# A conformer block in FP32-like precision: five FFN pairs and twelve down-projection tiles by Strassen's scheme

## The chip, the cores and the metric

The kernel runs on one core of a Trainium2 chip. The time is the device time of that core in microseconds for one execution; a run's number is the median of its executions. One execution of each kernel is also recorded by the hardware profiler, and all rows below are from that one. PE is TensorE, DVE is VectorE, ACT is ScalarE, POOL is GpSimd, SP is the engine that issues the DMAs.

## The reference

One layer: a conformer convolution mixer and then a gated conv-FFN, for one sequence of 1024 tokens by 1024 channels, FFN width 2816, all in float32. Cut to what matters:

```python
h = rmsnorm(x, norm_pre_mix) * (1 + sc_m) + sh_m
u = h @ w1 + b1;  a, gt = split(u);  u = a * sigmoid(gt)
u = causal_dwconv(u, dw_w) + dw_b                 # width 31
u = silu(layernorm(u, ln_g, ln_b));  y = u @ w2 + b2
x = x + gt_m * rmsnorm(y, norm_post_mix)
h = rmsnorm(x, norm_pre_ffn) * (1 + sc_f) + sh_f
u = causal_dwconv(h @ w_up, f_dw_w) + f_dw_b      # width 3
gt, v = split(u);  y = (silu(gt) * v) @ w_down
out = x + gt_f * rmsnorm(y, norm_post_ffn)
```

## The kernel before, in words

The tokens are two blocks (0 and 1) of 512. Activations lie channels on partitions, a tile being 128 channels by 512 tokens. Every large product is three matmuls (`mm3`, L256 to L258; `mm3g`, L627 to L629): each operand is split into a high half (rounded, L242 on ScalarE or L244 on VectorE) and a low half (the rest, L245 on VectorE or GpSimd), and high x high, high x low and low x high are added in PSUM. A weight tile is loaded to `raw` (three buffers), split into `W` (four buffers), and used.

The program's order is: modulation vectors and pointwise1 of block 0 with part of block 1; the width-31 depthwise convolution of block 0 (`conv`: taps in PSUM on VectorE, L353; seven taps go by ScalarE products L347 and GpSimd additions L351); its layer norm; pointwise2 of block 0; a shared pointwise1 tile of block 1; the transposes and modulation of block 0 (`modulate_block`, L265). Then the FFN of block 0: 12 tile pairs up (`up_pair`: 48 matmuls, the width-3 convolution L526 to L528, gate L535 and L536), the down projection of these 12 (`down_half`, ci 0), 10 more pairs, and the down projection of those (ci 1) in two halves of the output channels. Between the two halves stand block 1's layer norm (`ln_center` L403 and on, `ln_rstd` L429 to L437, `ln_swish` L444), pointwise2 of block 1 with its residual and norm (`pointwise2`, L458 to L478), and, inside the second half, block 1's transposes. Block 1's convolution, all on VectorE, runs beside block 0's FFN.

Block 1's FFN goes in three chunks (8, 8 and 6 tiles): the pairs of a chunk (`up_pair` with low halves on VectorE), for every two of them the four sums and differences of hidden-tile quarters (`hid_pair`, L611 to L614 on GpSimd), and the down projection by Strassen's scheme with seven products in place of eight (`down_strassen`; weight combinations L691 on VectorE; accumulators in SBUF, L656).

Each engine takes its instructions in a fixed order that the build decides; an instruction that waits holds back those behind it on its engine. Tile pools release a buffer when its last reader is done.

## Time and profile before

| | |
|---|---|
| runs shown | 1096.85 us median (1096.79 to 1172.39) |
| the profiled execution | 1097.28 us; span 1095.5, so 1.8 us lie around it |
| PE busy | 1065.0 us, 97% |
| DVE busy | 817.3 us, 75% |
| POOL busy | 524.1 us, 48% |
| ACT busy | 500.4 us, 46% |
| mean granted PE clock | 0.991 |
| DMA | 139 MB, 36.9% of 16 engines' span |

How to read it: a share of the span says how long an engine worked, not whether others waited for it. The chain of work that ended last says what the end hung on, the waits say what an engine's idle time ended with, and the timeline gives start and length of single instructions (a row with a count is several in a run). Matmuls overlap in the records, so their pace is read from start to start.

### The profile page before, as it was taken

The page shows a single profiled execution, that of the slowest core. Times are in us where ns is not written, and L with a number is a line of the kernel's source. Part 1 is how long each engine was busy: PE and PEld are TensorE (multiplying, and loading weights), DVE is VectorE, ACT ScalarE, POOL GpSimd, SP SyncE. Part 2 cuts the span into 40 slices and gives each one's busy share as a digit, 9 for nine tenths or more (in the row PEclk, how much of TensorE's full clock was granted, in tenths as well). Part 3 has the DMA queues.
Part 4 walks back from the last instruction along what each step waited for, and adds up shares of the span by engine and source line. Part 5 has one row for each costly group of instructions (what it writes and reads, how often), then busy time and mean ns, then how long its engine had stood idle before and what let it go on. Part 6 is the DMA issues. An engine that isn't in the chain of part 4 may idle for free.

```text
span 1095.5 us, 13048 instructions
## 1 busy us (share of the span) xinstructions
PE 1065.0 (97%) x4786; PEld 841.9 (77%) x4786; DVE 817.3 (75%) x1103; ACT 500.4 (46%) x774; POOL 524.1 (48%) x420
## 2 busy tenths in 40 slices
PE   5999999999899999999999999999999999999995
PEld 3778876778688888888887788888887888878873
DVE  3499989534799999989978673786596555965687
ACT  3595555453644544333434442445445444343453
POOL 1398877544734444443344363433267024640464
PEclk9999999999899999999999999999999999999998
DMA  9951135443422223342243353567204322043022
GB/s 369 369 193 58 58 116 192 154 135 104 146 75 90 87 97 96 97 173 97 96 151 100 96 154 96 173 211 270 97 20 154 115 97 96 19 135 109 26 77 77
DMA packets 41832, 139.01 MB, mean 127 GB/s; under 512 B 4644, under 2 KB 4644, under 8 KB 41768
## 3 DMA queue, kind: packets, MB, share of 16 engines
q1 hardware_dynamic: 41768, 138.18, 36.9%
q8 instruction: 37, 0.61, 0.2%
q14 instruction: 27, 0.22, 0.1%
HBM read 129.77 MB, written 8.39 MB: 126 GB/s over the span
## 4 chain that ended last, share of the span: by engine, by line
PE 89%; DVE 5%; POOL 2%; DMA 1%; ACT 1%; issue 1%; SPq 0%; POOLq 0%; DVEq 0%; ACTq 0%
PE bank L256 26%; PE bank L257 26%; PE bank L258 26%; PE bank L628 2%; PE bank L629 2%; PE bank L627 2%; DVE W L245 1%; PE bank L265 1%; PE bank L178 1%; DMA Y<-in_mod_ch 1%; DVE Y L473 1%; PE cbank L149 1%; DVE yacc L656 1%; DVE R L691 1%; DMA x2d<-Y 0%
## 5 line engine op out<-in xcount | busy, mean ns | idle before, releaser
L256 PE MATMUL bank<-A,W 128*128 128x512 f32 x960 | 379.6, 398 | 0.3 <-ACT U L267 0.3
L257 PE MATMUL bank<-A,W 128*128 128x512 f32 x960 | 379.2, 395 | 0.0
L258 PE MATMUL bank<-A,W 128*128 128x512 f32 x960 | 378.9, 395 | 0.0
L245 POOL TENSOR_TENSOR W<-raw,W 128x1024 fp32r<-128x1024 f32 x99 | 244.8, 2473 | 272.5 <-ACT W L242 230.3
L353 DVE SCALAR_TENSOR_TENSOR cbank<-U,vecs,cbank 128x512 f32<-128x512 f32 x424 | 290.8, 747 | 9.0 <-ACT cbank L341 7.8
L256 PEld LDWEIGHTS bank<-A,W 128*128 128x128 f32 x960 | 180.9, 189 | 48.5 <-DVE cbank L353 1.7
L258 PEld LDWEIGHTS bank<-A,W 128*128 128x128 f32 x960 | 180.9, 188 | 43.6 <-issue 0.8
L257 PEld LDWEIGHTS bank<-A,W 128*128 128x128 f32 x960 | 180.8, 188 | 43.4 <-issue 1.1
L242 ACT ACTIVATE W<-raw 128x1024 fp32r<-128x1024 f32 x150 | 158.0, 1053 | 110.1 <-PE bank L258 72.7
L526 ACT ACTIVATE U<-bank,vecs 128x512 f32<-128x512 f32 x88 | 68.4, 778 | 194.3 <-PE bank L258 184.6
L527 DVE SCALAR_TENSOR_TENSOR U<-bank,vecs,U 128x511 f32<-128x511 f32 x88 | 65.4, 745 | 80.2 <-ACT U L526 80.0
L256 PE MATMUL bank<-W,A 128*128 128x512 f32 x304 | 121.1, 398 | 0.0
L257 PE MATMUL bank<-W,A 128*128 128x512 f32 x304 | 120.2, 395 | 0.0
L258 PE MATMUL bank<-W,A 128*128 128x512 f32 x304 | 118.9, 395 | 0.0
L532 POOL TENSOR_TENSOR U<-U,hv 128x2 f32<-128x2 f32 x44 | 12.7, 289 | 155.9 <-DVE U L527 153.0
L245 DVE TENSOR_TENSOR W<-raw,W 128x1024 fp32r<-128x1024 f32 x51 | 62.2, 1221 | 16.4 <-ACT W L242 16.3
L245 DVE TENSOR_TENSOR A<-U,A 128x512 fp32r<-128x512 f32 x73 | 67.3, 933 | 8.3 <-ACT A L242 7.7
L351 POOL TENSOR_TENSOR Q<-Q,Q 128x512 f32<-128x512 f32 x48 | 62.2, 1296 | 15.9 <-ACT Q L347 14.9
L256 PEld LDWEIGHTS bank<-W,A 128*128 128x128 f32 x304 | 57.2, 188 | 13.7 <-DVE U L536 0.2
L257 PEld LDWEIGHTS bank<-W,A 128*128 128x128 f32 x304 | 57.2, 188 | 13.6 <-issue 0.5
L258 PEld LDWEIGHTS bank<-W,A 128*128 128x128 f32 x304 | 57.2, 188 | 13.5
L528 DVE SCALAR_TENSOR_TENSOR U<-bank,vecs,U 128x510 f32<-128x510 f32 x88 | 65.3, 744 | 1.6
(147 smaller groups left out, 1208.1 us busy)
## 6 DMA issues: line engine op xcount, KB each, us to landing
raw<-in_wup SPq DMA_DIRECT2D x88, 512.0 KB, 3.2
raw<-in_w SPq DMA_DIRECT2D x40, 512.0 KB, 3.9
Y<-in_mod_hp SPq DMA_DIRECT2D x32, 512.0 KB, 5.9
raw<-in_wdn SPq DMA_DIRECT2D x22, 512.0 KB, 3.5
R<-in_wdn SPq DMA_DIRECT2D x20, 512.0 KB, 3.7
Af<-in_mod_ch SPq DMA_DIRECT2D x12, 512.0 KB, 10.2
Y<-in_x SPq DMA_DIRECT2D x8, 512.0 KB, 10.0
U<-in_x SPq DMA_DIRECT2D x16, 256.0 KB, 3.9
```

The costliest lines, as they stand in the source:

```text
L242: nc.scalar.activation(dst[:, 0], src, AF.Copy)
L245: split_lo[0] = lo.tensor_tensor(dst[:, 1], src, dst[:, 0].bitcast(F32), op=ALU.subtract)
L256: nc.tensor.matmul(o, l[0], r[0], start=start, stop=False)
L257: nc.tensor.matmul(o, l[0], r[1], start=False, stop=False)
L258: nc.tensor.matmul(o, l[1], r[0], start=False, stop=stop)
L351: nc.gpsimd.tensor_tensor(acp, acp, q, op=ALU.add)
L353: nc.vector.scalar_tensor_tensor(acc, ut[:, k:k + 512], tap(k), acc, op0=ALU.mult, op1=ALU.add)
L526: nc.scalar.activation(t[:, :512], bk, AF.Identity, bias=V("fb", i), scale=wk[2])
L527: nc.vector.scalar_tensor_tensor(t[:, 1:512], bk[:, 0:511], wk[1], t[:, 1:512], op0=ALU.mult, op1=ALU.add)
L528: nc.vector.scalar_tensor_tensor(t[:, 2:512], bk[:, 0:510], wk[0], t[:, 2:512], op0=ALU.mult, op1=ALU.add)
L627: nc.tensor.matmul(o, l[0], r[0], start=start, stop=False, skip_group_check=group)
L628: nc.tensor.matmul(o, l[0], r[1], start=False, stop=False, skip_group_check=group)
```

## The change

It has five parts. (1) The convolution of block 1 gives nine of its taps to ScalarE and GpSimd, and two of its eight channel tiles are asked for ahead of the rest. (2) Block 0's FFN runs its first 10 pairs as before; their down projection goes to DRAM (`down_spill` into `yd`). Block 1's layer norm, pointwise2 and the operands for what follows (`both_operands`) come right after. (3) Pairs 15 to 19 are computed once for both blocks by seven products of 1024 x 512 halves (`up_both`: 84 matmuls), where a second up projection in block 1 fell away; their outputs go to DRAM (`hd`). (4) Tiles 10 to 14, 20 and 21 of block 0 go to DRAM too, and all 12 come back into `hid_pair` and two chunks of `down_strassen`, which add to `yd`. (5) Four pairs of block 1 are computed ahead, and block 1's chunks reload what is stored.

Lines of the changed file stand some ten higher: L353 becomes L363, L256 to L258 become L264 to L266, L245 is L253, L244 is L252, L265 is L273, L437 is L447, L444 is L454, L478 is L488, L611 to L614 are L602 to L605, L627 to L629 are L618 to L620.

```diff
-CHUNKS = ((0, 12), (12, 22))
+NSTD = 10
+BOTH = range(15, 20)
+CHUNKS0 = ((10, 16), (16, 22))
+AHEAD = 4
+EARLY = 2
+POOL_TAPS1 = 9
...
+    def down_spill(lo, hi, h, hid, lo_eng, yd):
         n = hi - lo
...
         ys = [bank() for _ in range(NT)]
...
+        for q in range(n // 2):
+            ww = weights(wdn[h, :, (lo // 2 + q) * 1024:(lo // 2 + q + 1) * 1024], lo_eng)
             for t in range(NT):
...
+                for e in range(2):
...
+                    mm3(ys[t], (a[:, 0, ts], a[:, 1, ts]), (ww[:, 0, sl], ww[:, 1, sl]), kk == 0, kk == n - 1)
+                if q == n // 2 - 1:
+                    y = tU()[:, :512]
+                    nc.scalar.copy(y, ys[t])
+                    nc.sync.dma_start(yd[t * P:(t + 1) * P, h * 512:(h + 1) * 512], y)
...
+    def both_operands(h2, xs, keep):
...
...
+        B = {"B11": h2[:4], "B21": h2[4:], "B22": [], "B1": [], "B2": [], "B3": [], "B4": []}
+        for k in range(4):
+            h11, h21 = h2[k].bitcast(F32), h2[k + 4].bitcast(F32)
+            x12 = modulate_T(xs, s_f, sh_f, k, hi=None)
+            nc.sync.dma_start(keep[k], x12)
+            x22 = modulate_T(xs, s_f, sh_f, k + 4, hi=None)
+            B["B22"].append(operand(x22, V, True))
+            t1, t2, t3, t4 = [tU()[:, :512] for _ in range(4)]
+            V.tensor_tensor(t1, x12, h11[:, 0], op=ALU.subtract)
+            V.tensor_tensor(t1, t1, h11[:, 1], op=ALU.subtract)
+            G.tensor_tensor(t3, x22, x12, op=ALU.subtract)
+            V.tensor_tensor(t2, x22, t1, op=ALU.subtract)
+            G.tensor_tensor(t4, h21[:, 0], t2, op=ALU.subtract)
+            G.tensor_tensor(t4, t4, h21[:, 1], op=ALU.add)
+            for n, x, lo in (("B1", t1, V), ("B2", t2, V), ("B3", t3, V), ("B4", t4, G)):
+                B[n].append(operand(x, lo))
+        return B
...
+    def up_both(jj, B, hd):
...
...
+        def operand(src, lo):
...
+            W = pw.tile([P, 2, 1024], F32R, tag="W", name=nm("W"))
+            split(W[:, :, :n], src, lo=lo)
+            return lambda o: lambda k: (W[:, 0, o + k * P:o + (k + 1) * P], W[:, 1, o + k * P:o + (k + 1) * P])
+        w1_ = operand(rg, V)
+        r12 = pr.tile([P, 1024], F32, tag="raw", name=nm("raw"))
+        G.tensor_tensor(r12[:, L], rv[:, L], rv[:, H], op=ALU.add)
+        G.tensor_tensor(r12[:, H], r12[:, L], rg[:, L], op=ALU.subtract)
+        w2_ = operand(r12, V)
+        G.tensor_tensor(rv[:, L], rg[:, L], rv[:, L], op=ALU.subtract)
+        w3_ = operand(rv, G)
+        G.tensor_tensor(rg[:, H], rg[:, H], r12[:, H], op=ALU.subtract)
+        w4_ = operand(rg[:, H], V)
+        ug, uv = [pm.tile([P, 1024], F32, tag=t, name=nm(t)) for t in ("ug", "uv")]
+        X, Z, Q = bank(), bank(), bank()
+        def product(o, w, Bs, start, group):
+            for k in range(4):
+                mm3g(o, w(k), (Bs[k][:, 0], Bs[k][:, 1]), start and k == 0, k == 3, group)
+        def add(y, o):
+            V.tensor_tensor(y, o, y, op=ALU.add)
+        product(X, w1_(0), B["B11"], True, True)
+        nc.scalar.copy(ug[:, L], X)
+        product(Z, w1_(512), B["B21"], True, False)
+        add(ug[:, L], Z)
+        product(X, w2_(512), B["B2"], False, True)
...
+        cv = []
+        for g, u_ in ((1, uv), (0, ug)):
+            i = g * NPAIR + jj
...
+            t = pm.tile([P, 1024], F32, tag="tv" if g else "tg", name=nm("t"))
+            nc.scalar.activation(t, u_, AF.Identity, bias=vec_("fb", i), scale=wk[2])
+            V.scalar_tensor_tensor(t[:, 1:], u_[:, :1023], wk[1], t[:, 1:], op0=ALU.mult, op1=ALU.add)
+            V.scalar_tensor_tensor(t[:, 2:], u_[:, :1022], wk[0], t[:, 2:], op0=ALU.mult, op1=ALU.add)
+            cv.append(t)
+        nc.scalar.activation(cv[1], cv[1], AF.Silu)
+        G.tensor_tensor(cv[1], cv[1], cv[0], op=ALU.mult)
+        nc.sync.dma_start(hd, cv[1])
...
+    yd = dr.tile([TB, D], F32, name="yd")
+    hd = {}
+    def spill(b, jj, h2, *how):
+        x = up_pair(b, jj, h2, *how, whole=False)
+        hd[b, jj] = dr.tile([P, 512], F32, name=f"hd_{b}_{jj}")
+        nc.sync.dma_start(hd[b, jj], x)
+    hid, gf = [], []
+    for jj in range(NSTD):
+        hid.append(up_pair(0, jj, h2))
+        if jj in (6, 8):
+            h = jj // 2 - 3
+            gf.append(row_sums(3, 1, h, piece_loads(3, h), g_f))
     for h in range(2):
...
+        down_spill(0, NSTD, h, hid, G, yd)
+    cs1 = [conv(1, j, POOL_TAPS1) for j in range(EARLY)]
     with tc.issue_after(after.ins):
...
+        cs1 += [conv(1, j, POOL_TAPS1) for j in range(EARLY, KD)]
+    cm, sq = ln_center(cs1)
+    r = ln_rstd(sq)
+    vs = ln_swish(cm, r)
+    for jj in range(NSTD, NSTD + 2):
+        spill(0, jj, h2)
+    xs = pointwise2(1, vs, b2, g_m, x2d)
+    right.close()
+    pat = right.enter_context(tc.tile_pool(name="pat", bufs=8, side="right", reuse_waits="tile"))
+    keep = [dr.tile([P, 512], F32, name=f"keep_{k}") for k in range(4)]
+    B = both_operands(h2, xs, keep)
     for f in gf:
         f()
...
+    for jj in range(NSTD + 2, BOTH[0]):
+        spill(0, jj, h2)
+    halo_terms(0, BOTH[0])
+    top.close()
+    pm = top.enter_context(tc.tile_pool(name="pm", bufs=2, reuse_waits="tile"))
+    for jj in BOTH:
+        d = dr.tile([P, 1024], F32, name=f"hd_{jj}")
+        up_both(jj, B, d)
+        for b in range(2):
+            hd[b, jj] = d[:, b * 512:(b + 1) * 512]
+    right.close()
+    pn = right.enter_context(tc.tile_pool(name="pn", bufs=8, side="right", reuse_waits="tile"))
+    def reload(src):
+        x = tU()[:, :512]
+        nc.sync.dma_start(x, src)
+        return x
+    h2b = []
+    for k in range(4):
+        a = tA()
+        split(a, reload(keep[k]))
+        h2b.append(a)
+    h2b += B["B22"]
+    for jj in range(BOTH[-1] + 1, NPAIR):
+        spill(0, jj, h2)
+    halo_terms(BOTH[-1] + 1, NPAIR)
+    top.close()
+    pn2 = top.enter_context(tc.tile_pool(name="pn2", bufs=3, reuse_waits="tile"))
+    def whole_down(b, chunks, tile_of, new):
+        yacc = [pn2.tile([P, 1024], F32, tag="yacc", name=nm("yacc"), bufs=NT) for _ in range(NT)]
+        if not new:
+            for t in range(NT):
+                nc.sync.dma_start(yacc[t], yd[t * P:(t + 1) * P, :])
+        for ci, (lo, hi) in enumerate(chunks):
+            n = hi - lo
+            ops, a11, raws = [], None, None
+            for p in range(n // 2):
+                if p == max(0, n // 2 - 2):
+                    raws = down_raw(lo, n)
+                sa, sb = tile_of(lo + p), tile_of(lo + n // 2 + p)
+                if p % 2 == 0:
+                    a11 = tA()
+                ops.append(hid_pair(sa, sb, a11, p % 2))
+            ready = split_hi[0]
+            last = ci == len(chunks) - 1
+            ns = [small(8, "n3") for _ in range(NT)] if last else None
+            down_strassen(new and ci == 0, lo, n, ops, raws, yacc, ns, finish(b, yacc, ns, x2d) if last else None)
+        return ready
+    ready = whole_down(0, CHUNKS0, lambda jj: reload(hd[0, jj]), False)
+    for jj in range(AHEAD):
+        spill(1, jj, h2b, DV, cbank)
+    with tc.issue_after(ready.ins):
+        whole_down(1, CHUNKS1, lambda jj: reload(hd[1, jj]) if (1, jj) in hd else up_pair(1, jj, h2b, DV, whole=False), True)
```

Where instructions stand, at three places. Rows are line, operation, destination, sources and shape in the changed or the former file; numbers name buffers.

TensorE before, at the end of block 1's pointwise2: the last product (L258, `A_5245` is the last tile of the norm), the down projection's matmuls (`bank_5584` to `bank_5587`), and the transposes of block 1 (L265, `Y_5248` to `Y_5251`).

```order
L257 MATMUL bank_5391<-W_5409,A_5245 128x512
L258 MATMUL bank_5391<-W_5409,A_5245 128x512
L256 MATMUL bank_5584<-W_5590,A_4234 128x512
...
L257 MATMUL bank_5587<-W_5648,A_4633 128x512
L258 MATMUL bank_5587<-W_5648,A_4633 128x512
L265 MATMUL bank_5685<-ident,Y_5248 128x128
L265 MATMUL bank_5685<-ident,Y_5249 128x128
L265 MATMUL bank_5685<-ident,Y_5250 128x128
L265 MATMUL bank_5695<-ident,Y_5248 128x128
```

TensorE now, at the same place: the last product of pointwise2 (L266), the transposes (L273, `Y_4396` to `Y_4399`), and the first pair behind them.

```order
L265 MATMUL bank_4539<-W_4557,A_4243 128x512
L266 MATMUL bank_4539<-W_4557,A_4243 128x512
L273 MATMUL bank_4750<-ident,Y_4396 128x128
L273 MATMUL bank_4758<-ident,Y_4396 128x128
...
L273 MATMUL bank_4870<-ident,Y_4399 128x128
L220 MATMUL bank_4902<-U_3158,ones 128x512
L220 MATMUL bank_4905<-U_3329,ones 128x512
L264 MATMUL bank_4918<-A_2544,W_4910 128x512
```

The 72 matmuls between projection and transposes are gone from there; the 32 transposes follow the projection directly.

VectorE now, at the second layer norm: the products with the norm's factor (L454, `cbank_4196` is what L447 broadcasts), a tap of pair 10 (L537), and the casts and the first subtraction (L252, L253) that TensorE's first product in pointwise2 (`A_4201`) reads.

```order
L454 TENSOR_TENSOR U_4198<-U_224_1407,cbank_4196 128x512
...
L454 TENSOR_TENSOR U_4240<-U_209_1319,cbank_4196 128x512
L537 SCALAR_TENSOR_TENSOR U_4306<-bank_4256,vecs,U_4306 128x511
L252 CAST A_4201<-U_4198 128x512
L252 CAST A_4207<-U_4204 128x512
...
L252 CAST A_4231<-U_4228 128x512
L538 SCALAR_TENSOR_TENSOR U_4306<-bank_4256,vecs,U_4306 128x510
L253 TENSOR_TENSOR A_4201<-U_4198,A_4201 128x512
```

Before, matmuls of `down_half` stood on TensorE while these ran; now TensorE's next 128x512 matmul behind L447 reads `A_4201`.

POOL now, at block 0's Strassen projection: weight low halves (`W_6101`, `W_6116`, L253) and behind them the sums of the reloaded tile pairs (L602 to L605) and their low halves (`A_6004` and on).

```order
L253 TENSOR_TENSOR W_6101<-R_6014,W_6101 128x1024
...
L253 TENSOR_TENSOR W_6116<-R_6022,W_6116 128x512
...
L602 TENSOR_TENSOR U_5998<-U_5988,U_5990 128x256
L603 TENSOR_TENSOR U_5999<-U_5988 128x256
...
L253 TENSOR_TENSOR A_6004<-U_5998,A_6004 128x512
L253 TENSOR_TENSOR A_6005<-U_5999,A_6005 128x512
...
L253 TENSOR_TENSOR A_6063<-U_6057,A_6063 128x512
...
L253 TENSOR_TENSOR W_6386<-R_6295,W_6386 128x1024
```

TensorE now, at the first matmuls of that projection: the last reader of the buffer that `W_6116` gets (`W_5898`, pair 21's), and the first product.

```order
L264 MATMUL bank_5902<-A_2614,W_5898 128x512
L265 MATMUL bank_5902<-A_2614,W_5898 128x512
L266 MATMUL bank_5902<-A_2614,W_5898 128x512
L618 MATMUL bank_6069<-W_6075,A_5992 128x512
L619 MATMUL bank_6069<-W_6075,A_5992 128x512
```

Before, block 0's second half used `down_half`, and no tile pair of block 0 came by these instructions.


## Rows read from the trace of the kernel before

**Rows 1.** The page: busy us (share) xinstructions by engine, and the chain.

```profile
PE 1065.0 (97%) x4786; PEld 841.9 (77%) x4786; DVE 817.3 (75%) x1103; ACT 500.4 (46%) x774; POOL 524.1 (48%) x420
...
PE 89%; DVE 5%; POOL 2%; DMA 1%; ACT 1%; issue 1%; SPq 0%; POOLq 0%; DVEq 0%; ACTq 0%
```

**Rows 2.** Waits of TensorE, longest sum: us in total, times, longest.

```profile
PE bank L265 <- DVE Y L284: 11.0, 4, 8.0
```

**Rows 3.** Timeline of TensorE: start, us, instruction, count, idle before.

```profile
799.62 0.40 PE L257 MATMUL bank<-A,W 128*128 128x512 f32 x1
...
815.26 0.39 PE L258 MATMUL bank<-A,W 128*128 128x512 f32 x1
```

**Rows 4.** Windows: length, busy us (x) of PE, PEld, DVE, ACT, POOL, PEclk, DMA, GB/s.

```profile
200.00:230.00 30.00, 29.90 (x185) 23.22 (x184) 9.09 (x24) 16.94 (x23) 14.56 (x14) 1.00 0.27 87
...
305.00:450.00 145.00, 145.00 (x625) 117.48 (x624) 143.51 (x204) 64.70 (x107) 63.08 (x26) 1.00 0.29 92
```

**Rows 5.** Timeline of VectorE: a cast, and then block 1's layer norm.

```profile
229.12 0.43 DVE L244 CAST A<-U 128x512 fp32r<-128x512 f32 x1 [4.29 <-ACT U L392]
...
626.15 3.68 DVE L444 TENSOR_TENSOR U<-U,cbank 128x512 f32<-128x512 f32 x6 [0.69 <-PE cbank L437]
...
631.54 1.99 DVE L244 CAST A<-U 128x512 fp32r<-128x512 f32 x1
```

**Rows 6.** Timeline of VectorE at the end of block 0's pointwise2.

```profile
273.50 0.69 DVE L458 TENSOR_TENSOR Y<-bank,b 128x512 f32<-128x512 f32 x1 [0.38 <-PE bank L258]
...
293.44 1.47 DVE L478 TENSOR_SCALAR Y<-Y,n 128x1024 f32<-128x1024 f32 x1 [2.35 <-DMA x2d<-Y]
```

**Rows 7.** Timeline of TensorE at block 0's transposes and first pair.

```profile
294.96 1.33 PE L265 MATMUL bank<-ident,Y 128*128 128x128 f32 x5 [0.82 <-DVE Y L478]
...
297.92 0.78 PE L256 MATMUL bank<-A,W 128*128 128x512 f32 x1
```

**Rows 8.** Timeline of POOL in the same stretch.

```profile
277.65 5.37 POOL L245 TENSOR_TENSOR W<-raw,W 128x1024 fp32r<-128x1024 f32 x2
```

**Rows 9.** Timeline of VectorE at the end of block 1's pointwise2.

```profile
691.90 0.69 DVE L458 TENSOR_TENSOR Y<-bank,b 128x512 f32<-128x512 f32 x1 [0.38 <-PE bank L258]
...
709.76 0.75 DVE L478 TENSOR_SCALAR Y<-Y,n 128x1024 f32<-128x1024 f32 x1 [1.54 <-DMA x2d<-Y]
```

**Rows 10.** Windows of 5 us at block 0's transposes.

```profile
290.00:295.00 5.00, 2.27 (x9) 1.47 (x9) 2.56 (x3) 3.64 (x5) 2.67 (x5) 0.58 0.63 210
295.00:300.00 5.00, 5.00 (x19) 4.48 (x20) 3.69 (x7) 4.53 (x7) 2.12 (x1) 0.50 0.30 105
```

**Rows 11.** Single lines: durations in ns min/median/max, first and last start.

```profile
L245 POOL TENSOR_TENSOR W<-R,W x16: 1291/2413/4803, 811.9 to 1068.1; 128x1024 fp32r<-128x1024 f32 x14, 128x512 fp32r<-128x512 f32 x2
...
L245 POOL TENSOR_TENSOR A<-U,A x30: 1286/1298/2311, 77.0 to 1062.5; 128x512 fp32r<-128x512 f32 x30
...
L611 POOL TENSOR_TENSOR U<-U,U x11: 731/742/1657, 752.7 to 1056.1; 128x256 f32<-128x256 f32 x11
...
L612 POOL TENSOR_TENSOR U<-U x11: 1183/1210/1774, 753.4 to 1057.1; 128x256 f32<-128x256 f32 x11
...
L527 DVE SCALAR_TENSOR_TENSOR U<-bank,vecs,U x88: 731/749/753, 312.1 to 1053.1; 128x511 f32<-128x511 f32 x88
...
L536 DVE TENSOR_TENSOR U<-U,U x44: 675/683/2898, 320.5 to 1054.7; 128x512 f32<-128x512 f32 x44
```

**Rows 12.** Timeline of VectorE and of POOL at a pair of block 1.

```profile
820.36 2.27 DVE L536 TENSOR_TENSOR U<-U,U 128x512 f32<-128x512 f32 x1
...
819.67 2.41 POOL L245 TENSOR_TENSOR W<-R,W 128x1024 fp32r<-128x1024 f32 x1
...
822.71 1.66 POOL L611 TENSOR_TENSOR U<-U,U 128x256 f32<-128x256 f32 x1 [0.63 <-DVE U L536]
...
828.84 2.55 POOL L245 TENSOR_TENSOR A<-U,A 128x512 fp32r<-128x512 f32 x2
```

**Rows 13.** DMA issues: KB each, us to landing.

```profile
U<-x2d SPq DMA_DIRECT2D x16, 256.0 KB, 3.0
```

More of the change, by code (lines that the diff above doesn't have):

```diff
@@ L510, in trunk_kernel, with up_pair @@
     hv = cst.tile([P, 2, NPAIR, 2], F32, name="hv")
[L512 removed]
+    def up_pair(b, jj, h2, lo_eng=nc.gpsimd, bank=bank, whole=True):
         cv = []
@@ L629, in mm3g, with operand @@
         nc.tensor.matmul(o, l[1], r[0], start=False, stop=stop, skip_group_check=group)
+    def both_operands(h2, xs, keep):
+        V, G = nc.vector, nc.gpsimd
+        spare = [pat.tile([P, 2, 512], F32R, tag="AT", name=nm("AT")) for _ in range(8)]
+        def operand(x, lo, held=False):
+            a = spare.pop() if spare and not held else tA()
+            split(a, x, lo=lo)
+            return a
+        B = {"B11": h2[:4], "B21": h2[4:], "B22": [], "B1": [], "B2": [], "B3": [], "B4": []}
[15 more added lines that the diff above has]
+        return B
@@ L652, in accumulate @@
             y = yacc[t][:, ds]
-            if first and ci == 0:
+            if first and new:
                 nc.scalar.copy(y, o)
```

121 lines of the change are left out of this document (38 added, 83 removed).

## Prediction

> **What bounds the kernel now.** I read the page first: TensorE is busy 1065.0 of 1095.5 us and the chain that ended last runs 89% through it [rows 1]. Then the waits by engine: TensorE's longest sum is 11.0 us at the start, before any FFN work [rows 2]. Third, the timeline of a stretch without a wait, for the price of a matmul: 67 of the 128x512 form start between 799.62 and 815.26, so 15.64/67 = 0.2333 us each [rows 3]. The kernel is a queue of some 4250 such matmuls, and everything else lies beside them. So the gain of the change is read off TensorE's instruction count, and its loss off each place where it has nothing ready.
>
> **The gain.** Of the 128x512 form the order has 4254 before and 4158 after. Five pairs take 84 matmuls for both token blocks in place of 2x48 (-60), and the block-0 down projection of 12 tiles takes 252 in place of 288 (-36). 96 x 0.2333 = 22.4 us, 2.0% of the time; there is no more to win. The sum starts at the profiled execution's 1097.28 us (0.4 above the median of 1096.85): 1097.3 - 22.4 = 1074.9 with every new piece of work hidden. What follows are five places where I looked for the cover.
>
> **1. Nine taps on GpSimd, two channel tiles early.** Vector taps fall from 424 to 352; 72 products go to ScalarE and 64 additions to GpSimd, which were busy 64.7 and 63.1 of the 145 us from 305 to 450 [rows 4]. Vector has 206 instructions between the last operand of block 0's up projection and the last product of block 1's convolution; before, 204 instructions of the same mix took the 145 us from 305 to 450 [rows 4], so it is done near 451. TensorE wants it after ten tiles and the down projection, 720 matmuls or 168 us from 297.92 [rows 7], at 466: hidden, with 15 us to spare; were the spare gone, each late microsecond would cost one. The 34 taps and one addition taken early (35 x 145/204 = 24.9 us) go into 200 to 230, where Vector is idle 30 - 9.1 = 20.9 us, in gaps between the steps of a norm that TensorE waits for [rows 4]. 24.9 - 20.9 puts the first cast 4.0 us late. I take **4** (1, if some of the taps come before 200, to 7).
>
> **2. The second layer norm.** It moves ahead of the pointwise projection with nothing between. Before, its products start at 626.15 and its first casts at 631.54 [rows 5], and TensorE ran down-projection matmuls throughout. Now TensorE's next 128x512 matmul behind the broadcast (L447) is the projection itself. Vector does eight products (six took 3.68, so 0.61 each, 4.9), one conv tap 0.75 [rows 11] and a cast 0.43 [rows 5] before the first matmul: 6.1 us. The third product wants the low half, which comes after five more casts, a tap and the subtraction (0.68, as L536), 5x0.43 + 0.75 + 0.68 = 3.6 us later, of which six matmuls cover 1.4. 6.1 + 3.6 - 1.4 = 8.3. I take **8** (6 to 11).
>
> **3. From the projection to its transposes.** This is the dearest. The transposes now stand directly behind the last projection matmul; before, 72 matmuls of the down projection (16.8 us) stood there. How long that gap is the trace tells twice. In block 0 Vector takes the last bank but one at 273.50, twelve matmuls (2.8) before TensorE is through, so at 276.3; the fourth normalised tile is done at 293.44 + 1.47 = 294.9, 18.6 us later [rows 6]. TensorE idled little there because 48 matmuls of a shared convolution tile (11.2 us) filled it, and it still waited 0.82 for the last tile [rows 7]. Part of the 18.6 is two weight splits on GpSimd (5.37 us) in the middle of the root chain [rows 8]; in the changed order two such splits stand there again, behind the third tile's first root. In block 1 the same walk is from 691.90 + 2.8 = 694.7 to 709.76 + 0.75 = 710.5: 15.8 us, with four weight splits of 1.2 us on Vector [rows 9]. Of this the 24 transposes of the earlier tiles can run, some 6 us at the rate of five in 1.33 [rows 7], where the clock was low, and 3 on the full clock: 18.6 - 6 and 15.8 - 3 are both 13. After such gaps the clock is lower: granted 0.58 and then 0.50 over two 5 us windows, TensorE busy throughout the second [rows 10], where 0.50 is 1.2 GHz and 1.00 is 2.4 GHz; half of 5 us of work is lost there and a little behind it, 3. I take 13 + 3 = **16** (11 to 20).
>
> **4. Operands and steady state of the five double pairs.** Each of four k-steps gives Vector and GpSimd new differences and splits: by the changed order 31 us on GpSimd to the last operand, priced at 1.30 for a 128x512 and 2.41 for a 128x1024 split [rows 11]. Beside it stand three ordinary pairs, 144 matmuls or 33.6 us. Cover without contention is whole, 0; the 28 Vector operations with two inputs in SBUF, 0.68 each as L536 [rows 11], 19 us, laid end to end with the 31 would overrun 33.6 us and the 5.6 of the first pair's products that need no late operand by 11. I take **3** (0 to 11). In the steady state a pair needs 84 matmuls, 19.6 us, against about 10 each of Vector, ScalarE and GpSimd: 0.
>
> **5. Block 0's Strassen projection.** Two chunks, 252 matmuls, 58.8 us, come back to back, with no up projection between them to hide their operands; before, the two block-1 pairs beside each operand gave 96 matmuls. On GpSimd the split of W_6116 waits for a weight buffer that TensorE's last matmul ahead of the chunk releases, and behind it in the queue stand the operands of all six tile pairs. A pair costs three halves of the kind of L611 at 0.74, one of L612 at 1.21 and two splits at 1.30, together 6.0 us [rows 11], six 36.1; the weight splits up to W_6386 are 3x2.41 + 3x1.29 = 11.1; four small halo products about 1. Together 48.2 us from the chunk's first matmul, when the buffer comes free, and TensorE wants W_6386 144 matmuls on, at 33.6: late by **14.6**. A point on the way agrees: A_6063 is there after 21.7 and wanted after 14.7. That is the price if GpSimd runs at its undisturbed durations. It did not at 822.71: the same pair took from there to 831.39, 8.7 us in place of 6.0, while Vector worked on SBUF operands; and a Vector product of 0.68 took 2.27, ending half a microsecond behind GpSimd's 2.41 split [rows 12]. With every instruction stretched by 8.7/6.0 the list takes 70, and the lateness is 36. I take **20**, nearer the lower end, since Vector's operations with PSUM input keep their time (88 of them, longest 0.753) [rows 11] and of the rest only a part meets GpSimd.
>
> The Trainium skill, page "SBUF — State Buffer", section "SBUF: two separate sides", states it as a rule: Vector and GpSimd share a port pair as an exclusive lock, which a Vector operation with two SBUF inputs holds against a GpSimd operation that reads SBUF, and the other one blocks fully. By that rule places 4 and 5 go to the upper ends, 11 and 36, and the sum to 1150. The trace bears it out where the two meet (2.27 for 0.68), and leaves open how often they do.
>
> The new DRAM traffic (11 single and 5 double tile outputs stored, 21 loads, 8 stores and 4 loads of the accumulators, 4 operands out and back) is asked for tens of matmuls ahead of its use; a 256 KB load lands in 3.0 us [rows 13], 13 matmuls: 0. Block 1's last chunk is denser on GpSimd: 0, up to 6.
>
> **Sum.** 1074.9 + 4 + 8 + 16 + 3 + 20 = **1126**, 2.7% slower.
>
> **Rivals.** (A) *The matmul count decides.* If the five places were covered, 1075, on the faster side: 2.0% under. It needs place 3 covered, and TensorE has nothing else in its queue there; I see no way for more than half of it. 0.03. (B) *Floors.* Every place at its lower end, 1 + 6 + 11 + 0 + 14.6 = 32.6: 1107.5, 0.9% slower and no measurable difference. For it: GpSimd's undisturbed durations are the common ones; place 3 could lose the two splits if they happen to come early. It turns into my case when the stalls pass 44, which is 1119. 0.32. (C) *Full lock between Vector and GpSimd*: 1074.9 + 4 + 8 + 16 + 11 + 36 = 1150. For it: the stretched rows at 822; against: the median of L536 is 0.683 with a longest of 2.898, so most keep their time [rows 11]. 0.15. The forecast itself 0.50.
>
> **How the numbers follow.** A measurement of this kernel can tell about 2% from no change: faster is below 1075, slower above 1119. (A) at 1075 sits on that line and gives faster 0.03. Of the forecast's own 0.50 a tenth, 0.05, ends below 1119, since places 1, 3 and 5 can each come out some 5 shorter. Same: 0.32 + 0.05 = 0.37; slower: 0.45 + 0.15 = 0.60. The range takes in (B)'s floor with some 10 us for work that I count as late and is not, and (C) at its top: 1097 to 1152.
>
> **What would show it.** The matmul count in the profile after, 4158 at 0.233. Place 3: one or two TensorE idle rows ahead of the 128x128 transposes in block 1, released by Vector's normalisation, of 9 to 17 us together, and a granted clock near 0.5 just behind. Place 2: TensorE idle some 6 us ahead of the first projection matmul and some 2 more at its third, released by Vector's cast and split. Place 5: idle rows on the Strassen lines released by GpSimd's splits, 15 to 36 in all, and GpSimd at nine tenths or more in that stretch. Place 1: the first cast behind block 0's norm some 4 us later in its stage. The forecast is wrong if TensorE is idle under 30 us more than before in these five places together (the operands were ready earlier than their queues say), or if an idle time appears that is not on the list, above all a convolution of block 1 that is not done when the norm wants it.

## The result and the profile after

The changed kernel takes 1169.65 us (median) against 1096.82: 1.0669 times as long, 95% interval 1.0653 to 1.0685. It is slower by 72.8 us. (The ratio compares fast runs alone; one of the four of the kernel before, 1172.39 us, is left out of it.) The forecast had the direction, most of the places, and less than half of the size: 1126, at most 1152.

The page of the changed kernel, busy time by engine and the chain by engine [rows 1]:

```profile
PE 1074.2 (92%) x4690; PEld 838.2 (72%) x4690; DVE 889.7 (76%) x1094; ACT 575.8 (49%) x885; POOL 723.7 (62%) x557
...
PE 59%; DVE 20%; POOL 8%; issue 6%; ACT 3%; DMA 2%; SPq 0%; POOLq 0%; DVEq 0%; ACTq 0%
```

The chain of work that ended last ran 89% through TensorE before and runs 59% through it now; VectorE has 20% of it for 5%, GpSimd 8% for 2%. TensorE's waits, which before had one entry over 4 us [rows 2], by line and releaser, us in total, times, longest:

```profile
PE bank L618 <- ACT A L596: 11.8, 2, 6.6
PE bank L273 <- DVE Y L294: 10.8, 4, 7.9
PE bank L273 <- DVE Y L488: 9.6, 5, 4.2
PE bank L619 <- POOL W L253: 6.8, 3, 5.4
PE bank L264 <- DVE A L252: 6.0, 1, 6.0
PE bank L273 <- ACT bank L469: 5.2, 1, 5.2
PE cbank L264 <- DVE U L538: 4.6, 1, 4.6
PE bank L264 <- DVE g_f L221: 3.8, 1, 3.8
PE bank L220 <- ACT U L275: 3.6, 1, 3.6
PE bank L382 <- ACT Y L392: 3.0, 1, 3.0
```

The second entry was there before (11.0), and the third with 3.5 in place of 9.6; the others were not. To put the loss in place I took the start of the same step in both traces and subtracted 0.2333 us for each 128x512 matmul of a product between two starts. Start and duration of TensorE's rows at the seams, first block 1's first pair in the kernel before, and then the changed kernel:

```profile
725.90 0.40 PE L256 MATMUL bank<-A,W 128*128 128x512 f32 x1
```

```profile
240.84 0.67 PE L264 MATMUL bank<-W,A 128*128 128x512 f32 x1
...
309.99 0.80 PE L264 MATMUL bank<-A,W 128*128 128x512 f32 x1 [0.16 <-ACT U L275]
...
518.38 0.79 PE L264 MATMUL bank<-W,A 128*128 128x512 f32 x1 [5.96 <-DVE A L252]
...
596.06 0.79 PE L264 MATMUL bank<-A,W 128*128 128x512 f32 x1 [3.75 <-DVE g_f L221]
...
756.76 0.80 PE L618 MATMUL bank<-W,A 128*128 128x512 f32 x1 [5.16 <-ACT A L596]
...
838.62 0.39 PE L264 MATMUL cbank<-A,W 128*128 128x512 f32 x1
...
891.65 0.39 PE L265 MATMUL bank<-A,W 128*128 128x512 f32 x1
...
1154.22 0.39 PE L620 MATMUL bank<-W,A 128*128 128x512 f32 x1
```

| stretch | how | lost more than before | forecast |
|---|---|---|---|
| to block 0's first pair (place 1) | 309.99 - 297.92 [rows 7] | 12.1 | 4 |
| pairs, norm, pointwise2, transposes of block 1, to pair 12 (places 2, 3, 4) | 286.1 - 1008 x 0.2333 = 50.9; before 725.90 - 297.92 - 1776 x 0.2333 = 13.6 | 37.3 | 27 |
| pairs 12 to 14, double pairs, 20, 21 | 160.7 - 660 x 0.2333, less the wait of 5.2 | 1.5 | 0 |
| block 0's Strassen projection (place 5) | 5.16 + 81.86 - 252 x 0.2333 | 28.2 | 20 |
| the four pairs of block 1 behind it | 53.0 - 199 x 0.2333 (seven are the next pair's) | 6.6 | 0 |
| the rest of block 1 | 262.8 - 1079 x 0.2333 = 11.1; before 355.8 - 1518 x 0.2333 = 1.6 | 9.5 | 0 |

Together 95.2, less the 22.4 won by 96 matmuls fewer: 72.8. The spans differ by 72.5 (1168.0 - 1095.5), since what follows the last matmul is 0.3 shorter. The stretches cover the whole span, so the sum closes however it is cut; what it checks is the 96 matmuls and their pace.

### The profile page after: what moved, and what is told of

Its sections match the earlier page's. It is cut to its first block, busy times and chain, and to the rows that moved or that the text cites. A ratio compares the mean times of both kernels' runs of the same rounds, so it can differ in the third digit from the quotient of the medians.

```text
span 1168.0 us, 13296 instructions
## 1 busy us (share of the span) xinstructions
PE 1074.2 (92%) x4690; PEld 838.2 (72%) x4690; DVE 889.7 (76%) x1094; ACT 575.8 (49%) x885; POOL 723.7 (62%) x557
## 4 chain that ended last, share of the span: by engine, by line
PE 59%; DVE 20%; POOL 8%; issue 6%; ACT 3%; DMA 2%; SPq 0%; POOLq 0%; DVEq 0%; ACTq 0%
PE bank L264 12%; PE bank L266 12%; PE bank L265 12%; PE bank L619 5%; PE bank L620 5%; PE bank L618 5%; DVE cbank L363 4%; POOL W L253 3%; DVE W L253 2%; DVE R L773 2%; DVE Y L483 2%; DVE U L546 1%; DVE A L253 1%; PE cbank L264 1%; PE cbank L266 1%
## 5 line engine op out<-in xcount | busy, mean ns | idle before, releaser
L253 POOL TENSOR_TENSOR W<-raw,W 128x1024 fp32r<-128x1024 f32 x87 | 214.7, 2471 | 143.4 <-ACT W L250 143.3
L264 PE MATMUL bank<-A,W 128*128 128x512 f32 x736 | 293.2, 401 | 4.5 <-DVE g_f L221 3.8
L265 PE MATMUL bank<-A,W 128*128 128x512 f32 x736 | 292.8, 398 | 0.0
L266 PE MATMUL bank<-A,W 128*128 128x512 f32 x736 | 291.4, 397 | 0.0
L363 DVE SCALAR_TENSOR_TENSOR cbank<-U,vecs,cbank 128x512 f32<-128x512 f32 x352 | 241.6, 747 | 5.0 <-ACT cbank L351 4.1
L250 ACT ACTIVATE W<-raw 128x1024 fp32r<-128x1024 f32 (+1 forms) x138 | 143.2, 1038 | 84.5 <-PE bank L266 49.5
L361 POOL TENSOR_TENSOR Q<-Q,Q 128x512 f32<-128x512 f32 x112 | 155.1, 1385 | 36.9 <-ACT Q L357 34.5
L264 PEld LDWEIGHTS bank<-A,W 128*128 128x128 f32 x736 | 139.5, 190 | 46.6 <-DVE g_f L221 5.3
L266 PEld LDWEIGHTS bank<-A,W 128*128 128x128 f32 x736 | 139.7, 190 | 33.9 <-issue 1.1
L265 PEld LDWEIGHTS bank<-A,W 128*128 128x128 f32 x736 | 139.9, 190 | 32.5 <-issue 0.2
L357 ACT ACTIVATE Q<-U,vecs 128x512 f32<-128x512 f32 x128 | 90.7, 719 | 65.8 <-POOL Q L361 58.9
L618 PE MATMUL bank<-W,A 128*128 128x512 f32 x238 | 92.0, 411 | 15.1 <-ACT A L596 11.8
L619 PE MATMUL bank<-W,A 128*128 128x512 f32 x238 | 96.6, 409 | 9.3 <-POOL W L253 6.8
L620 PE MATMUL bank<-W,A 128*128 128x512 f32 x238 | 93.0, 408 | 3.8 <-DVE A L253 2.9
L264 PE MATMUL bank<-W,A 128*128 128x512 f32 x208 | 83.9, 405 | 6.9 <-DVE A L252 6.0
L250 ACT ACTIVATE W<-R 128x1024 fp32r<-128x1024 f32 x70 | 64.6, 927 | 47.9 <-PE bank L620 28.0
L250 ACT ACTIVATE A<-U 128x512 fp32r<-128x512 f32 x85 | 52.2, 629 | 63.9 <-DVE U L546 28.5
L265 PE MATMUL bank<-W,A 128*128 128x512 f32 x208 | 83.7, 402 | 0.0
L266 PE MATMUL bank<-W,A 128*128 128x512 f32 x208 | 80.8, 401 | 0.0
L253 DVE TENSOR_TENSOR A<-U,A 128x512 fp32r<-128x512 f32 x73 | 70.3, 977 | 8.5 <-ACT A L250 8.1
```

What stands on the lines that cost most here:

```text
L250: split_hi[0] = nc.scalar.activation(dst[:, 0], src, AF.Copy)
L253: split_lo[0] = lo.tensor_tensor(dst[:, 1], src, dst[:, 0].bitcast(F32), op=ALU.subtract)
L264: nc.tensor.matmul(o, l[0], r[0], start=start, stop=False)
L265: nc.tensor.matmul(o, l[0], r[1], start=False, stop=False)
L266: nc.tensor.matmul(o, l[1], r[0], start=False, stop=stop)
L357: nc.scalar.activation(q, ut[:, k:k + 512], AF.Copy, scale=tap(k))
```

## The experiments

Each kernel ran once with a profile, beside the kernel before (1095.7 to 1096.6 us). The four times of the changed kernel lie between 1168.33 and 1171.38, so a total that differs from it by under 3 us tells nothing. The loss within a stretch repeats better: at place 5 it is 28.2 in the changed kernel, and 28.1 and 28.0 in e_early0 and e_cover, which leave that place as it is.

### Place 1: the convolution inside block 0's norm

**b_taps**: the kernel before with the convolution's part alone.

```diff
+    cs1 = [conv(1, j, 9) for j in range(2)]
     with tc.issue_after(after.ins):
-        cs1 = [conv(1, j) for j in range(KD)]
+        cs1 += [conv(1, j, 9) for j in range(2, KD)]
```

> The kernel before with the convolution part of the change alone: nine taps of block 1's convolution on ScalarE and GpSimd, two channel tiles ahead of the rest. Theory (the early taps stand in the norm's gaps): block 0's pointwise2 starts 9 us later and all is slower by 9 to 12: 1106 to 1109. Rival (the loss there comes from the rest of the change, buffers or DMA): 1097, no change.

Measured: 1109.87, 13.6 slower, a little over what the theory gave. The first pair starts 13.3 late (311.21 for 297.92) and behind it nothing is lost.

**b_held**: the same nine taps, no tile early, and ScalarE's products also held back. `issue_after` orders only the engine of the instruction that it is given, here VectorE; this adds ScalarE's.

```diff
-    with tc.issue_after(after.ins):
-        cs1 = [conv(1, j) for j in range(KD)]
+    with tc.issue_after(after.ins), tc.issue_after(after_act.ins):
+        cs1 = [conv(1, j, 9) for j in range(KD)]
```

> The kernel before with nine taps of block 1's convolution on ScalarE and GpSimd, no channel tile early, and ScalarE's products held behind block 0's modulation as VectorE's taps are. Theory (the 13 us of the taps alone come from convolution work of VectorE, ScalarE and GpSimd inside block 0's norm and pointwise2, not from the taps' work as such): 1095 to 1099, and the first up matmul within 2 us of 297.92. Rival (GpSimd's additions cost TensorE operands also behind that point): 1103 and up.

Measured: 1096.42, no change. Nine taps on GpSimd cost nothing; where they run costs 13 us. Two things differ between the two kernels, the early tiles and the products; e_early0 tells them apart. TensorE at the first pair, b_taps and then b_held:

```profile
311.21 0.50 PE L256 MATMUL bank<-A,W 128*128 128x512 f32 x1 [0.16 <-ACT U L267]
```

```profile
297.85 0.48 PE L257 MATMUL bank<-A,W 128*128 128x512 f32 x1
```

**e_early0**: the changed kernel with no tile early, the products not held.

```diff
-EARLY = 2
+EARLY = 0
```

> The changed kernel, with no channel tile of block 1's convolution ahead of the rest (EARLY 0 for 2). Theory: its taps in the gaps of block 0's norm cost the 9.4 us by which pointwise2 of block 0 starts later than in the kernel before (240.84 against 231.39), and 1.6 more by the lower clock behind it; without them pointwise2 starts near 231.5 and the first up matmul of block 0 near 298. The convolution of block 1 then has 25 us more to do behind that point: if VectorE bounds it, it ends near 490, some 20 us later in its stage than TensorE wants it, and the gain is given back there: 1165 to 1180. Rival: it is hidden by ups 10 and 11 and by GpSimd's own pace, and the whole falls by 8 to 11, to about 1159.

Measured: 1186.01, worse than either theory. Pointwise2 of block 0 starts at 236.23: of the 9.4 us by which it was late, the two early tiles make 4.6, and the products and additions that nothing holds back the rest. The first pair starts at 305.20, so 7.3 of the 12.1 us of place 1 are left (in the other kernels that keep this place it starts between 308.4 and 312.0). The convolution then ends late, though not by VectorE: it waits 10.11 us for GpSimd's additions before its last instruction, and TensorE is idle 11.4 us at block 1's norm and 3.7 within it, in two pieces. VectorE in e_early0, and then the same instruction in the changed kernel:

```profile
508.34 0.69 DVE L365 TENSOR_TENSOR U<-cbank,Q 128x512 f32<-128x512 f32 x1 [10.11 <-POOL Q L361]
```

```profile
480.65 0.69 DVE L365 TENSOR_TENSOR U<-cbank,Q 128x512 f32<-128x512 f32 x1 [8.60 <-POOL Q L361]
```

The prediction had it done at 451 by VectorE's count; VectorE's own taps end 8.60 before the second row, at 472.1, and GpSimd sets the end, at 480.65. In the changed kernel that was still in time: TensorE has pairs 10 and 11 beside the norm and waits nowhere for it. The kernel before had the convolution done at 540.6 and read it 50 us later; the changed one reads it as it comes. The norm's first matmuls, before and then changed:

```profile
590.15 1.92 PE L403 MATMUL cbank<-U,first 128*32 128x512 f32 x16
```

```profile
479.57 2.88 PE L413 MATMUL cbank<-U,first 128*32 128x512 f32 x16
```

### Places 3 and 4: from pointwise2 to the double pairs

**e_cover**: pairs 12 to 14 in front of the transposes. **e_cover5**: 20 and 21 too.

```diff
+    for jj in range(NSTD + 2, BOTH[0]):        # e_cover5: and 20, 21
+        spill(0, jj, h2)
     B = both_operands(h2, xs, keep)
     for f in gf:
         f()
-    for jj in range(NSTD + 2, BOTH[0]):
-        spill(0, jj, h2)
...
-    for jj in range(BOTH[-1] + 1, NPAIR):      # e_cover5 alone
-        spill(0, jj, h2)
```

> The changed kernel with pairs 12 to 14 (144 matmuls, 33.6 us) ahead of the transposes of block 1, where they stood behind them. Theory (cover): TensorE's 18.7 us idle between projection and first pair go, and the operands of the double pairs, which those pairs covered, are late instead by 10 to 20: total 1150 to 1162. Rival (the operands are not covered at all, 30 us or more): no gain or slower, 1168 and up.

Measured: 1167.29, a miss, and too near the changed kernel to call better. The 18.7 us idle between projection and pair 12 went, and 15 came back behind the transposes: these stand behind all 144 matmuls on TensorE, so the operands, which begin with them, got no cover at all. TensorE in e_cover:

```profile
610.69 3.63 PE L220 MATMUL bank<-U,ones 128*128 128x512 f32 x4 [5.85 <-ACT U L275]
619.09 0.79 PE L618 MATMUL bank<-A,W 128*128 128x512 f32 x1 [4.77 <-DVE g_f L221]
633.41 0.80 PE L619 MATMUL bank<-A,W 128*128 128x512 f32 x1 [4.06 <-DVE A L253]
```

> The changed kernel with pairs 12 to 14 and also 20 and 21 (240 matmuls, 56 us) ahead of the transposes of block 1. Theory: the norm behind pointwise2 and the operands of the double pairs are both hidden, the stage loses its 18.7 us idle and the low clock behind it, some 22 to 25 us: 1145 to 1148, if block 0's Strassen chunk waits as long as now (28). Rival: pairs 20 and 21 covered part of that chunk's operands, and it waits up to 22 us longer: 1165 to 1170.

Measured: 1171.20, no difference from the changed kernel; just above the rival's range, but hardly for its reason. The Strassen chunks, which follow the double pairs without pairs 20 and 21, lose 29.5 us where they lost 28.2. It is the operands that wait, as in e_cover: from the projection to the double pairs 18 us are lost in place of 31, and in the double pairs, where nothing was lost, 12.

**e_split**: 12 and 13 in front of the transposes, row sums ahead of them, and 14, 20 and 21 behind.

```diff
+    for jj in range(NSTD + 2, BOTH[0] - 1):
+        spill(0, jj, h2)
+    for f in gf:
+        f()
     B = both_operands(h2, xs, keep)
-    for f in gf:
-        f()
-    for jj in range(NSTD + 2, BOTH[0]):
+    for jj in [BOTH[0] - 1, *range(BOTH[-1] + 1, NPAIR)]:
         spill(0, jj, h2)
...
-    for jj in range(BOTH[-1] + 1, NPAIR):
-        spill(0, jj, h2)
```

> The changed kernel with pairs 12 and 13 (96 matmuls, 22.4 us) between block 1's pointwise2 and its transposes, the row sums ahead of the transposes, and pairs 14, 20 and 21 (33.6 us) behind them. Theory (both things behind pointwise2 can be hidden, the norm of some 18 us and the operands of some 37, if each has its own matmuls): TensorE's 18.7 us of idle there and the low clock behind it go, some 24: 1144 to 1149. Rival (pairs 20 and 21 are missed where they stood, ahead of block 0's Strassen chunk): that chunk waits 10 to 20 longer, 1155 to 1168.

Measured: 1163.58, the rival's size. From the projection's end (566.5) to the double pairs (635.2) are 68.7 us for 240 matmuls (56.0): 12.7 beside them, where the changed kernel has 65.0 for 144, 31.4. So 18.7 us are won there, and one wait stays, for ScalarE's first modulation:

```profile
600.11 0.79 PE L264 MATMUL bank<-A,W 128*128 128x512 f32 x1 [5.75 <-ACT U L275]
```

From there to the end of the Strassen chunks 42 us are lost in place of 28. The rival put these into the chunks; they lose only 3 more (31). The other 11 are lost in the double pairs, which lost nothing in the changed kernel: the longest waits there are 3.14 for GpSimd's split of a weight and 2.01 for a sum of VectorE's. Among the three orders that I tried, what one place won another lost in the main: the pairs that can cover something are too few.

### Place 5: block 0's Strassen projection

The loss here in the changed kernel is 28.2 us, counted from the last matmul of pair 21.

**e_nosums**: without the sums of a tile pair and their splits (the second tile's halves stand in for them).

```diff
+        if not sums:                            # block 0
+            return {"A11": at(a11, 256 if odd else 0), "A12": at(a2, 0), "A22": at(a2, 256),
+                    "S1": at(a2, 0), "S2": at(a2, 256), "S3": at(a2, 0), "S4": at(a2, 256)}
         f = [tU()[:, :512] for _ in range(2)]
```

> The changed kernel without the four sums of a tile pair and their splits on GpSimd (and ScalarE) for block 0's six pairs: the second tile's halves are used in their place. Theory (GpSimd's list of 48 us is what the chunks wait for): at most 5 us are lost there, and the total is 1142 to 1147. Rival (the reload from DRAM, the weight buffers or VectorE bound the chunks): 15 us or more are still lost there, 1155 and up.

Measured: 1149.83, 19.8 better, between the two and nearer the theory, which allowed 5 us of loss. From 753.1 to 820.9 are 67.9 us for 58.8: 9.1 lost. Most of it is one wait of 5.17 that has nothing to do with GpSimd. TensorE in e_nosums, and ScalarE ahead of the same matmul in the changed kernel:

```profile
758.23 0.71 PE L622 MATMUL bank<-W,A 128*128 128x512 f32 x1 [5.17 <-ACT A L596]
```

```profile
756.23 0.16 ACT L540 COPY halo<-bank 128x2 f32<-128x2 f32 x1 [1.59 <-DVE U L538]
756.29 0.42 ACT L596 ACTIVATE A<-U 128x256 fp32r<-128x256 f32 x1
```

ScalarE's split of the first operand (L596) stands behind the halo copy of pair 21 (L540), which waits for VectorE's convolution of that pair. But most of the wait is older. TensorE is through with pair 21 at 751.6; the first two stored tiles are asked for at 749.81, on SyncE's queue behind the store of pair 20, and take 5.4 us, to about 755.2. SyncE in the changed kernel, and these two loads as DMA issues:

```profile
748.97 0.32 SPq L923 DMA_DIRECT2D hd<-U  x1
...
749.81 0.95 SPq L962 DMA_DIRECT2D U<-hd  x2
```

```profile
U<-hd SPq DMA_DIRECT2D x2, 256.0 KB, 5.4
```

The other long wait that is put down to L596 in the changed kernel, 6.59 at 771.08, is gone in e_nosums: in the changed kernel ScalarE stands at that time behind splits that wait for GpSimd's sums (2.83 and 1.42).

**e_nocomb**: without VectorE's weight combinations in the two chunks.

```diff
         def combine(out, a, b):
-            V.tensor_tensor(out, a, b, op=ALU.subtract)
+            if new_:                            # block 1
+                V.tensor_tensor(out, a, b, op=ALU.subtract)
```

> The changed kernel without VectorE's weight combinations (subtractions of two SBUF tiles, 16 instructions) in block 0's two Strassen chunks: the raw weights are used in their place. Theory (VectorE and GpSimd keep each other out of SBUF): GpSimd's list there runs nearer its undisturbed durations and the chunks lose 12 to 18 us by waiting, not 28: 1152 to 1160; an operand wait is left since the list alone is 14.6 late. Rival (no such exclusion; VectorE's own length bounds): GpSimd's durations stay as they are, stalls fall by the one 5.4 us wait behind a combination: 1164.

Measured: 1165.31, 4.3 better, nearer the rival's 1164; the chunks lose 23.6 us in place of 28.2. The 12 splits of operands on GpSimd there took 16.9 us in place of 20.2 (1.41 each, 1.68 with the combinations; 1.30 undisturbed [rows 11]). The two engines do hold each other up, and the combinations' part in it is worth some 4.6 of the 28. VectorE's splits, which also read two tiles in SBUF, were still there, so this is not the whole worth. Where it shows most, VectorE and GpSimd of the changed kernel:

```profile
802.69 9.49 DVE L773 TENSOR_TENSOR R<-R,R 128x1024 f32<-128x1024 f32 x4
```

```profile
802.18 5.63 POOL L253 TENSOR_TENSOR A<-U,A 128x512 fp32r<-128x512 f32 x3
807.77 3.32 POOL L253 TENSOR_TENSOR W<-R,W 128x1024 fp32r<-128x1024 f32 x1
```

Four combinations, three of 1.21 and one of half the width and 0.68 when undisturbed (4.31), take 9.49; three splits of 1.30 take 5.63, and the weight split behind them is what TensorE then waits 5.36 for.

**e_dsums**: the sums on VectorE.

```diff
-        G = nc.gpsimd
+        G = eng or nc.gpsimd                   # VectorE for block 0
```

> The changed kernel with the four sums of each of block 0's six tile pairs on VectorE, their splits still on GpSimd. Theory (GpSimd's list is the bound): it is 20 us shorter (3.4 a pair), VectorE has room for the 10 it gets, and the chunks lose 12 to 18 in place of 28: 1153 to 1160. Rival (VectorE and GpSimd take turns in SBUF, so that moving work between them changes nothing): 1165 to 1172.

Measured: 1168.15, the rival's size. 56 us from the first operands on, by length, PE, PEld, DVE, ACT and POOL busy, first the changed kernel and then e_dsums:

```profile
755.00:811.00 56.00, 40.01 (x146) 30.03 (x146) 42.07 (x40) 25.06 (x40) 55.80 (x47) 0.88 0.33 109
```

```profile
758.00:814.00 56.00, 44.56 (x162) 32.83 (x162) 54.85 (x68) 24.39 (x40) 34.36 (x23) 0.91 0.35 108
```

GpSimd was busy 55.8 of 56 us; with the sums moved VectorE is busy 54.9 of 56, and of TensorE's waits in the chunks (16.6 us) VectorE ends 9.4. So the full engine is now the other one, and the chunks still lose 26.3. Some of its time is stretch, five combinations of 1.21 averaging 1.65, so the run does not tell a full engine from two that take turns.

**e_ahead**: the four block-1 pairs in front of both chunks. **e_order**: two pairs for each chunk, between its operands and its products.

```diff
+    for jj in range(AHEAD):                     # e_ahead
+        spill(1, jj, h2b, DV, cbank)
     ready = whole_down(0, CHUNKS0, lambda jj: reload(hd[0, jj]), False)
-    for jj in range(AHEAD):                     # e_ahead, e_order
-        spill(1, jj, h2b, DV, cbank)
...
             ready = split_hi[0]
+            if b == 0:                          # e_order
+                for jj in range(2 * ci, 2 * ci + 2):
+                    spill(1, jj, h2b, DV, cbank)
```

> The changed kernel with the four block-1 pairs (192 matmuls, 44.8 us) ahead of block 0's two Strassen chunks, not behind them. Theory (the chunks wait for operands that GpSimd makes, and any matmuls ahead of them cover these): the 28 us lost there fall to 5 to 12, and the total to 1147 to 1154, unless the four pairs' own wait of 4.6 for a bank stays. Rival (the waits are made by GpSimd's pace within the chunks, so that cover ahead does not help): 1165 to 1170.

Measured: 1162.57, 7.1 better, between the two: that is the loss in the four pairs (6.6), which goes; the chunks still lose 25.9. GpSimd in e_ahead, where the four pairs run from 751 to 796 and the products start at 798.6:

```profile
792.64 2.40 POOL L253 TENSOR_TENSOR W<-R,W 128x1024 fp32r<-128x1024 f32 x1 [4.56 <-ACT W L250]
...
798.33 1.29 POOL L253 TENSOR_TENSOR W<-R,W 128x512 fp32r<-128x512 f32 x1
799.58 0.91 POOL L602 TENSOR_TENSOR U<-U,U 128x256 f32<-128x256 f32 x1
```

GpSimd had hardly any work for 45 us, and the first sum (L602) still starts behind the weight split, when the pairs are over: the pairs stand ahead of the operands in the program's order. The stored tiles themselves are asked for only behind the last pair's store. SyncE in e_ahead:

```profile
789.92 0.33 SPq L923 DMA_DIRECT2D hd<-U  x1
790.34 1.81 SPq L962 DMA_DIRECT2D U<-hd  x4
```

> The changed kernel with two block-1 pairs between the operands of each of block 0's Strassen chunks and its products, in the program's order operands, pairs, products, so that the sums stand on GpSimd's queue ahead of the weight splits that wait for a buffer. Theory (queue position, not pace alone: four pairs ahead of everything gave only 2, since the sums still stood behind the weight split): the 28 us lost there and the 7 in the four pairs fall to 8 to 15 together: 1142 to 1150. Rival (pace): 1160 to 1166 as with the pairs ahead.

Measured: 1148.17, 21.5 better, as the theory said. From 749.85 to 868.28 are 118.4 us for 444 matmuls (103.6): 14.8 lost in place of 28.2 + 6.6, and the first sum starts at 759.37, released by its load:

```profile
759.37 0.74 POOL L602 TENSOR_TENSOR U<-U,U 128x256 f32<-128x256 f32 x1 [5.02 <-DMA U<-hd]
```

The work is the same and on the same engines. What differs is that the operands are asked for ahead of the pairs, whose 45 us now lie beside them.

### All places at once

**a_fix3h**: no tile early and the products held; pairs 10 to 12 ahead of the norm and 13 inside it; 14 and 15 and the row sums behind pointwise2; 16, 20 and 21 behind the transposes; three double pairs; e_order's place for the block-1 pairs.

```diff
-EARLY = 2
+EARLY = 0
-BOTH = range(15, 20)
+BOTH = range(17, 20)
...
-    with tc.issue_after(after.ins):
+    with tc.issue_after(after.ins), tc.issue_after(after_act.ins):
...
+    with tc.issue_after(mm_mu[0].ins):          # behind the norm's mean
+        spill(0, 13, h2)
```

> The changed kernel with all places filled as far as its matmuls reach: no early channel tiles and the products held; pairs 10 to 12 ahead of block 1's norm and 13 inside it; 14 and 15 behind pointwise2; 16, 20 and 21 behind the transposes; three double pairs, not five (24 matmuls more, 5.6 us); the block-1 pairs between operands and products of block 0's chunks. Theory (each loss is an uncovered wait): of the 95 us lost some 35 stay, 1097.3 - 16.8 + 35 = 1115, 1108 to 1125. Rival (the losses move on to the next operand because the engines, not the order, are short of time): 1135 and up.

Measured: 1144.87, a miss, on the rival's side. The loss at place 1 is gone (first pair at 298.1), and from the projection to the double pairs 13.7 us are lost in place of 31.4. But the convolution, no longer begun early, is late for block 1's norm, and the norm has little beside it. TensorE:

```profile
511.62 1.91 PE L415 MATMUL cbank<-U,first 128*32 128x512 f32 x2 [8.59 <-DVE U L367]
...
538.66 2.05 PE L449 MATMUL cbank<-U,ones 128*128 128x512 f32 x2 [4.31 <-DVE U L446]
...
546.67 0.79 PE L266 MATMUL bank<-W,A 128*128 128x512 f32 x1 [5.96 <-DVE A L254]
```

From the last down matmul (467.4) to pointwise2 (546.7) are 79 us for four pairs (44.8). No version that I ran beats the kernel before.

## Why the prediction was wrong, point by point

The step that failed most is the two zeros: the four pairs of block 1 and the rest of block 1 were put at nothing and lost 16.1 us, so that idle times appeared which were not on the list. At each of the other places a term of the sum was too small, by 8 to 10 us each; which one is told place by place.

**The gain** was right: 96 matmul records fewer (4690 for 4786), at 0.2333 where nothing waits.

**Place 1** (4; 12.1): the step that failed prices the gaps from 200 to 230 by VectorE alone, 24.9 us of early taps into 20.9 idle. What it prices is right: by e_early0 the early tiles cost 4.6, for 4.0. But the products on ScalarE and the additions on GpSimd, which the prediction put into the stretch from 305 to 450, also came before 305, since only VectorE was held; they make the rest, and b_held shows that with them held and no tile early nothing is lost. The same count missed GpSimd as the bound of the convolution: done at 481, not at 451. The prediction had the numbers for that. The kernel before spent 1.30 on such an addition, by its page (busy us, mean ns):

```profile
L351 POOL TENSOR_TENSOR Q<-Q,Q 128x512 f32<-128x512 f32 x48 | 62.2, 1296 | 15.9 <-ACT Q L347 14.9
```

The 64 additions are then 83 us, and with the 63.1 that GpSimd was busy already they are 146, for the 145 of the stretch (an estimate).

**Places 2 to 4** (27; 37.3): the waits were right in sum, 25.3 us where the prediction had 24, though not each in its place. Ahead of pointwise2 they are 6.6, 5.96 of it for the cast as forecast (8); the 2 us at the third product came out as 0.46. Ahead of the transposes they are 11.3 (13). The other 7.4 stand at the two row sums between the transposes and pair 12: these wait for a bank that ScalarE releases (3.65), and pair 12 for one that their reader on VectorE (L221) releases (3.75), both behind operands of the double pairs. The prediction looked for these operands at the double pairs (3), where nothing waited. The term that failed in size is the lower clock, which it charged once, 3 us: the other 12.0 are nearly all longer steps. The 32 transposes of block 1 took 7.6 us where they took 3.0 in the kernel before, the row sums 3.5 for 1.3, and the first 19 matmuls of products behind the waits 8.8 for 4.4, nearly all at a granted clock of 0.50 (1.2 GHz). The granted clock of the changed kernel by windows, length and busy us as in [rows 4], the clock behind POOL's figure:

```profile
500.00:520.00 20.00, 13.83 (x59) 8.49 (x55) 9.09 (x19) 8.59 (x11) 5.79 (x3) 0.85 0.23 73
...
580.00:600.00 20.00, 11.30 (x32) 6.94 (x31) 17.43 (x17) 10.74 (x17) 12.52 (x9) 0.69 0.13 48
...
760.00:780.00 20.00, 13.17 (x45) 9.89 (x44) 12.87 (x14) 10.48 (x18) 19.92 (x19) 0.74 0.32 105
```

Behind the long waits matmuls run at half the pace, and pointwise2 of block 1 takes 48.0 us for 192 matmuls (44.8). Counted from start to start over the products' matmuls without a wait, 17.6 us are lost at a granted clock of 0.50 in the changed kernel (89 steps) and 1.5 in the kernel before (7).

**Place 5** (20; 28.2): the list of 48.2 us on GpSimd, late by 14.6, was right as a floor. It began at 755.09, 3.5 us behind the buffer's release, and ran 56.0 us, 1.16 times its undisturbed length; 14.6 + 3.5 + 7.8 is 25.9, which is how late TensorE is when it goes on at 811.15. A last wait of 0.63 and the lower clock make the other 2.3. The term of 20 thus allowed 5.4 for a late start and a longer list, which are 11.3. What the prediction did not have is the 5.16 ahead of the first product. It put the reloads at 0, as "asked for tens of matmuls ahead"; the first two are asked for 1.8 us, some eight matmuls, before pair 21 ends. That wait lies beside the list and so adds little, but it is left when the list is gone (e_nosums).

**Rival (C)**, the full lock with its 36 at place 5, is not what happened: it needed every instruction stretched by 1.45, and the list was stretched by 1.16. The rule of the Trainium skill (page "SBUF — State Buffer", section "SBUF: two separate sides") agrees with the trace where the two engines meet, 9.49 for 4.31. Of what it costs here e_nocomb shows the combinations' part, 4.6 us; the rest is not shown.

**The two zeros** (0; 16.1). The four pairs of block 1 behind the chunks wait 4.63 for a bank whose reader, VectorE's convolution, stands behind block 0's closing work; e_ahead, which moves the pairs, loses that wait and all of the 6.6; in e_order 2.17 of the wait is left. The rest of block 1 has fewer matmuls between its chunks than before (192, 336 and 96, for 384, 384 and 288), and TensorE waits there for splits (2.5, 1.9). In a_fix3h, whose second chunk has 384 again, that chunk's projection takes 40.9 us, near the kernel before (40.3) and not 44.8. The third chunk does not fit: with 144 in a_fix3h it takes 36.0 us, with 96 in the changed kernel 31.8, with 288 before 29.6. So the cause of these 9.5 us is shown in part at most.

**The range** failed with the sizes: every place erred to the same side. My reading, which no run tests, is that each was priced as one wait beside otherwise undisturbed neighbours.
